# Hybrid RG-LRU and attention layer: the recurrent stage's gate multiplies and one-minus on VectorE, its input scaling on ScalarE

## The chip, the cores and the metric

The kernel runs on one core of one Trainium2 chip. The metric is device time in microseconds of one execution, the median of several runs. The profile is one execution on the chip, taken by the hardware profiler.

Names of engines, as the profile has them: PE is TensorE's matmul (PEld its weight loads), DVE is VectorE, ACT is ScalarE, POOL is GpSimd, SP is SyncE, which issues the DMAs here.

## What is computed

One layer, 4096 prompt positions and 8 single sample positions, model width 1024, all in float32:

```python
xn   = rms_norm(x, norm_pre)
proj = xn @ w_in            # columns: x_rnn 512 | g_rnn 512 | q 512 | k 128 | v 128 | g_att 512
xc   = causal_conv(x_rnn, width 4)
r, i = sigmoid(block-diagonal maps of xc)         # 8 blocks of 64
log_a = -8 * r * softplus(-lam);  a = exp(log_a)
h_t  = a_t * h_{t-1} + sqrt(1 - a_t^2) * (i_t * xc_t)
rnn_out = h * silu(g_rnn)
att_out = sliding_window_attention(q, k, v, ...) * silu(g_att)   # window 128, 8 query heads, 2 kv heads
y    = x + rms_norm(concat(rnn_out, att_out) @ w_out, norm_post)
```

## The kernel before, in words

There are three stages. Stage A (to about 480 us) normalises x, transposes it, projects the columns of x_rnn and g_rnn and runs the recurrence. Stage B (to about 1095 us) projects q, k, v and g_att and does the attention. Stage C is the output projection. Stage A and stage B overlap at their border, where the last chunks of A and the first weights and keys of B are worked at once.

Positions go in 11 chunks of 384 (the last has 256 and the 8 samples). x is held transposed, features on the 128 partitions, positions along the free axis. Each float32 product is made of three matmuls in a rounded float32 type, high by high, high by low and low by high (`mm3`, L122 to L124); so the weights and x are split into a high part (`wh`, `xh`) and a low part (`wl`, `xl`).

For one chunk `ci` stage A does, with `c` for one of four groups of 128 recurrent channels:

- `load_A(ci + 1)` (L145): three tiles `xs` of 128 rows by 1024 are loaded (L153; four buffers, three of which a chunk uses, so the second and third tile of a chunk wait until the chunk before has been transposed to the end); ACT squares and sums each (`sq`, L161); DVE adds eps (L136); POOL takes the power -1/2 (L141); then `xs` is scaled by that number per row (L166).
- `prep_A` (L170): PE transposes `xs` block by block (`pt`, L176, eight of them per chunk, three transposes each); ACT and DVE split the result into `xh` and `xl` (L179, L180), which are also stored for stage B.
- `proj_A` (L289): 48 matmuls give the channel and its gate (`pr_<ci>_<c>_1` and `_2`); the four PSUM tiles of tag "mm" hold two such pairs. ACT reads the first one out twice (`xr` L298, `xc` L302), DVE makes the convolution (L304, three per group), splits it (`xk`, L312 and L313), and makes the gate (`sg`, L318, after ACT's L316). Until ACT's L302 has read a tile, PE can't start the pair after the next in it.
- `rnn_A` (L321): six matmuls with the block-diagonal maps (`gt`), then ACT's L333, L334, L337, L338 and DVE's L339, L341, L342 and, between them, the one-minus `aa` (L340).
- `scan_A` (L345): once per chunk, ACT loads another function table and takes one square root over all four groups (`uu`, L348); then per group a multiply `ix *= uu` (L350), the scan on DVE (L352), a small copy of the last column (L355), the gate multiply `hh *= sg` (L361), and a store (L362).

The order of the program's text for one chunk is a list, `A_ORDER` (L32): P1 L P0 P2 R1 X0 R0 P3 X1 R2 X2 R3 S X3, with P for proj_A, R for rnn_A, X for two steps of prep_A of the next chunk, L for load_A of the next chunk and S for scan_A. That is not the order in which the engines get their instructions: the program is built under `tile.TileContext(nc, schedule_with_timeline_sim=True)` (L885), whose scheduler places every engine's instructions by its own model of their times. Each engine then works through its instructions in the order that the scheduler gave. So an edit of one line can shift the instructions of all the engines.

Of the kernel before, what the change touches and what calls it, by code (L numbers as in the profile page):

```python
# [12 lines left out]
AF = mybir.ActivationFunctionType  # L13
ALU = mybir.AluOpType
# [30 lines left out]
def hymba_kernel(ctx: ExitStack, tc: tile.TileContext, ins, outs):  # L45
    nc = tc.nc
# [14 lines left out]
    act = nc.scalar.activation  # L61
# [16 lines left out]
    def ps_s(n):  # L78
        if phase[0] == "A":
            return ps[1].tile([P, 1024], F32, tag="s", name=n, bufs=1)  # L80
        return ps[0].tile([P, 1024], F32, tag="s", name=n, bufs=2)
# [39 lines left out]
    def mm3(out, wh, wl, xh, xl, first, last):  # L121
        nc.tensor.matmul(out, wh, xh, start=first, stop=False)  # L122
        nc.tensor.matmul(out, wh, xl, start=False, stop=False)  # L123
        nc.tensor.matmul(out, wl, xh, start=False, stop=last)  # L124
# [10 lines left out]
    def rstd(pool, ss, rows, n):  # L135
        nc.vector.tensor_scalar(ss[:rows], ss[:rows], EPS, None, op0=ALU.add)  # L136
        return root(pool, ss, rows, n)

    def root(pool, ss, rows, n):
        rs = pool.tile([P, 1], F32, tag="rs", name=f"rs_{n}", bufs=4)  # L140
        nc.gpsimd.tensor_tensor(rs[:rows], ss[:rows], mhalf[:rows], op=ALU.pow)  # L141
        return rs


    def load_A(pool, ci):  # L145
        t0, npt, ns = chunks[ci]
        tiles = [(x_p[t0 + i * P:t0 + (i + 1) * P, :], P, i * P) for i in range(npt // P)]
        if ns:
            tiles.append((x_s, ns, npt))
        xn = []  # L150
        for j, (src, rows, off) in enumerate(tiles):
            xs = pool.tile([P, D], F32, tag="xs", name=f"xs_{ci}_{j}", bufs=4)
            nc.sync.dma_start(xs[:rows], src)  # L153
            ss = pool.tile([P, 1], F32, tag="ss", name=f"ss_{ci}_{j}", bufs=4)
            if ci == 0 and j == 1:
                sq = pal.tile([P, D], F32, tag="uu", name=f"sq_{ci}_{j}", bufs=1)
                nc.vector.tensor_tensor_reduce(sq[:rows], xs[:rows], xs[:rows], op0=ALU.mult, op1=ALU.add,
                                               scale=1.0 / D, scalar=0.0, accum_out=ss[:rows])
            else:
                sq = pool.tile([P, D], mybir.dt.bfloat16, tag="sq", name=f"sq_{ci}_{j}", bufs=1)  # L160
                act(sq[:rows], xs[:rows], AF.Square, scale=1.0 / 32.0, accum_out=ss[:rows])  # L161
            rs = rstd(pool, ss, rows, f"{ci}_{j}")
            if ci == 0:
                nc.vector.tensor_scalar(xs[:rows], xs[:rows], rs[:rows], None, op0=ALU.mult)
            else:
                nc.gpsimd.tensor_scalar(xs[:rows], xs[:rows], rs[:rows], 1.0, op0=ALU.mult, op1=ALU.mult)  # L166
            xn.append((xs, rows, off))
        return xn

# [28 lines left out]
    cms = [tc.tile_pool(name=n, bufs=1) for n in ("pa_late", "pa", "prep")]  # L198
    pal, pa, prep = [c.__enter__() for c in cms]
    xn = load_A(prep, 0)  # L200

    def project2(w1, w2, xs, W, n, wait=False):
# [118 lines left out]
    def rnn_A(pool, ci, c, uu, xc, xk, sg):  # L321
        t0, npt, ns = chunks[ci]
        W = npt + ns
        pg = ps_s(f"gt_{ci}_{c}")
        for g in range(2):
            o = pg[:, g * 512:g * 512 + W]
            mm3(o, gwh[:, 2 * c + g, :], gwl[:, 2 * c + g, :], xk[:, 0, :W], xk[:, 1, :W], True, True)

        def wt(tag, bufs=2, pool=pool):
            return pool.tile([P, STEP], F32, tag=tag, name=f"{tag}_{ci}_{c}", bufs=bufs)[:, :W]  # L330

        thr, thi = wt("thr", 3, pal), wt("thi", 4, pal)
        act(thr, pg[:, 0:W], AF.Tanh, scale=0.5, bias=hba[:, c:c + 1])  # L333
        act(thi, pg[:, 512:512 + W], AF.Tanh, scale=0.5, bias=hbx[:, c:c + 1])  # L334

        tt, aa = wt("tt", 2, pal), wt("aa", 4, pal)
        act(tt, thr, AF.Tanh, scale=sp2[:, c:c + 1], bias=sp2[:, c:c + 1])  # L337
        act(thr, thr, AF.Exp, scale=sp4n[:, c:c + 1], bias=sp4n[:, c:c + 1])  # L338
        nc.vector.scalar_tensor_tensor(thr, thr, 1.0, tt, op0=ALU.add, op1=ALU.mult)  # L339
        nc.gpsimd.tensor_scalar(aa, thr, -1.0, 1.0, op0=ALU.mult, op1=ALU.add)  # L340
        nc.vector.scalar_tensor_tensor(uu[:, c, :W], thr, 2.0, thr, op0=ALU.subtract, op1=ALU.mult)  # L341
        nc.vector.scalar_tensor_tensor(thi, thi, 1.0, xc[:, :W], op0=ALU.add, op1=ALU.mult)  # L342
        return aa, thi, sg

    def scan_A(pool, ci, uu, parts):  # L345
        t0, npt, ns = chunks[ci]
        W = npt + ns
        act(uu[:, :, :W], uu[:, :, :W], AF.Sqrt, scale=-0.25)  # L348
        for c, (aa, ix, sg) in enumerate(parts):
            nc.gpsimd.tensor_mul(ix, ix, uu[:, c, :W])  # L350
            hh = pal.tile([P, STEP], F32, tag="hh", name=f"hh_{ci}_{c}", bufs=4)
            nc.vector.tensor_tensor_scan(hh[:, :npt], aa[:, :npt], ix[:, :npt], hprev[c] if ci else 0.0,  # L352
                                         op0=ALU.mult, op1=ALU.add)
            hprev[c] = const.tile([P, 1], F32, tag=f"hl{c}", name=f"hl_{ci}_{c}", bufs=2)
            nc.gpsimd.tensor_copy(hprev[c], hh[:, npt - 1:npt])  # L355
            if ns:
                o = hh[:, npt:W]
                nc.vector.tensor_mul(o, aa[:, npt:W], h0T[:, c, :])
                nc.vector.tensor_add(o, o, ix[:, npt:W])
                nc.gpsimd.tensor_copy(hs[:, c, :], o)  # L360
            nc.gpsimd.tensor_mul(hh[:, :W], hh[:, :W], sg[:, :W])  # L361
            nc.sync.dma_start(mix_d[ci][:, c, :], hh[:, :W])  # L362


# [76 lines left out]
    for ci in range(NCH):  # L441
        for item in A_ORDER:
            f, s = item[0], st[ci]
            c = int(item[1:] or 0)
            if f == "P":
                s["p", c] = proj_A(pa, ci, c, wA, s["x"])
            elif f == "R":
                if "uu" not in s:
                    s["uu"] = pal.tile([P, 4, STEP], F32, tag="uu", name=f"uu_{ci}", bufs=1)
                s["r", c] = rnn_A(pa, ci, c, s["uu"], *s["p", c])  # L450
            elif f == "S":
                scan_A(pa, ci, s["uu"], [s["r", c] for c in range(4)])
            elif ci + 1 < NCH:
                if f == "L":
                    s["n"] = load_A(prep, ci + 1)
                else:
                    x = st[ci + 1].setdefault("x", ([], []))
                    prep_A(ci + 1, s["n"], (2 * c, 2 * c + 1), x)
        if ci == 3:
            setup_bias(pa)  # L460
# [314 lines left out]
    for ci in range(NCH):  # L775
# [14 lines left out]
        for j, (xsrc, ydst, rows, off) in enumerate(tiles):  # L790
# [52 lines left out]
            rs = root(const, ss[:, 0:1], rows, f"c{n}")  # L843
# [56 lines left out]
```

## Time and profile before

| | |
|---|---|
| runs | 1454.05, 1455.19, 1452.31 us, median 1454.05 |
| the profiled execution | 1454.09 us, of which its span is 1452.4 us |
| mean granted TensorE clock | 0.988 of full |
| busy over the span | PE 1408.3 us (97%), DVE 908.6 (63%), ACT 798.7 (55%), POOL 604.6 (42%) |
| chain that ended last, by engine | PE 83%, DVE 5%, ACT 4%, DMA 3%, issue 3%, POOL 1% |

The span is the time between the first and the last recorded instruction; 1.7 us of the execution lie outside it. An engine's busy time is the union of its instructions. The page prints the span in 40 slices, in tenths of busy time (9 is 90% or more), of which stage A is the first 13 or so:

```
PE   6999999999988889999999999999999999999998
DVE  5788777777878756576575575575665445334433
ACT  4656656666645566766776776776864222222211
POOL 3366665555656633544543543543762000000000
```

### The profile page before, as it was taken

The numbers are of one execution on the slowest core, as the hardware profiler recorded it, in microseconds if no ns is written. First come the engines' busy times: TensorE is split into PE (matmuls) and PEld (weight loads), VectorE is DVE, ScalarE is ACT, GpSimd is POOL, SyncE is SP. The second block draws the span as 40 slices with busy tenths as digits, with TensorE's granted clock in tenths as the row PEclk, the third lists the DMA queues.
The fourth block names the chain that finished last, engine by engine and source line by source line (L and its number), as shares of the span: only waits on it lengthen the run. The fifth ranks groups of instructions, "written<-read, shape, count | busy, mean of one in ns | idle before, by whom it ended". The sixth has DMA issues, their size and how long they took to land.

```text
span 1452.4 us, 24152 instructions
## 1 busy us (share of the span) xinstructions
PE 1408.3 (97%) x8127; PEld 1326.6 (91%) x8127; DVE 908.6 (63%) x2108; ACT 798.7 (55%) x2055; POOL 604.6 (42%) x1026
## 2 busy tenths in 40 slices
PE   6999999999988889999999999999999999999998
PEld 5999999999988889999999999999988888888886
DVE  5788777777878756576575575575665445334433
ACT  4656656666645566766776776776864222222211
POOL 3366665555656633544543543543762000000000
PEclk9999999999999999999999999999999999999999
DMA  8343354443324520221212212212336534433431
GB/s 271 127 157 133 131 168 148 142 152 120 122 73 145 184 79 31 99 85 67 99 46 76 98 42 79 98 38 70 107 111 196 172 131 145 141 135 131 146 130 60
DMA packets 115029, 170.24 MB, mean 117 GB/s; under 512 B 12214, under 2 KB 98822, under 8 KB 114906
## 3 DMA queue, kind: packets, MB, share of 16 engines
q1 hardware_dynamic: 114906, 168.71, 34.6%
q8 instruction: 64, 1.05, 0.3%
q14 instruction: 59, 0.48, 0.1%
HBM read 100.19 MB, written 68.50 MB: 116 GB/s over the span
## 4 chain that ended last, share of the span: by engine, by line
PE 83%; DVE 5%; ACT 4%; DMA 3%; issue 3%; POOL 1%; SPq 1%; POOLq 0%; DVEq 0%; ACTq 0%
PE out L817 8%; PE out L818 8%; PE out L819 8%; PE pr L122 6%; PE pr L124 6%; PE pr L123 6%; PE pga L122 4%; PE pga L123 4%; PE pga L124 4%; PE pq L122 4%; PE pq L123 4%; PE pq L124 4%; PE po L661 3%; PE S L601 2%; PE S L602 2%
## 5 line engine op out<-in xcount | busy, mean ns | idle before, releaser
L123 PE MATMUL pr<-xl,wh_in 128*128 128x384 f32 (+1 forms) x688 | 231.6, 337 | 0.0
L124 PE MATMUL pr<-xh,wl_in 128*128 128x384 f32 (+1 forms) x688 | 228.9, 334 | 0.0
L122 PE MATMUL pr<-xh,wh_in 128*128 128x384 f32 (+1 forms) x688 | 218.7, 336 | 0.9 <-ACT xc L302 0.6
L817 PE MATMUL out<-wh_out,xh_mix_d 128*128 128x512 f32 (+1 forms) x520 | 201.0, 387 | 0.0
L818 PE MATMUL out<-wl_out,xh_mix_d 128*128 128x512 f32 (+1 forms) x520 | 200.9, 386 | 0.0
L819 PE MATMUL out<-wh_out,xl_mix_d 128*128 128x512 f32 (+1 forms) x520 | 200.9, 386 | 0.0
L141 POOL TENSOR_TENSOR rs_c<-ssc,mhalf 128x1 f32<-128x1 f32 (+1 forms) x33 | 20.4, 620 | 322.5 <-DVE ssc L840 294.6
L836 ACT ACTIVATE sqc<-out 128x512 bf16<-128x512 f32 (+2 forms) x67 | 39.2, 585 | 194.6 <-PE out L819 184.4
L627 ACT ACTIVATE tt<-tt,nm 128x129 f32<-128x129 f32 x256 | 100.0, 393 | 77.2 <-DVE nm L624 76.7
L839 DVE TENSOR_TENSOR out<-out,gpost 128x512 f32<-128x512 f32 (+1 forms) x65 | 45.4, 698 | 144.2 <-ACT sqc L836 143.6
L123 PEld LDWEIGHTS pr<-xl,wh_in 128*128 128x128 f32 x688 | 131.3, 191 | 0.7 <-issue 0.7
L122 PEld LDWEIGHTS pr<-xh,wh_in 128*128 128x128 f32 x688 | 129.8, 191 | 2.1 <-ACT xc L302 1.8
L124 PEld LDWEIGHTS pr<-xh,wl_in 128*128 128x128 f32 x688 | 131.2, 191 | 0.3 <-issue 0.2
L122 PE MATMUL pq<-xh_B,wh_in 128*128 128x384 f32 (+1 forms) x352 | 119.5, 339 | 7.7 <-DVE kt L486 4.8
L123 PE MATMUL pga<-xl_B,wh_in 128*128 128x384 f32 (+1 forms) x352 | 119.1, 338 | 0.0
L123 PE MATMUL pq<-xl_B,wh_in 128*128 128x384 f32 (+1 forms) x352 | 118.9, 338 | 0.0
L124 PE MATMUL pq<-xh_B,wl_in 128*128 128x384 f32 (+1 forms) x352 | 118.6, 337 | 0.0
L304 DVE SCALAR_TENSOR_TENSOR xc<-xr,cT,xc 128x384 f32<-128x384 f32 (+1 forms) x132 | 113.0, 862 | 8.6 <-ACT xc L302 5.9
L122 PE MATMUL pga<-xh_B,wh_in 128*128 128x384 f32 (+1 forms) x352 | 118.3, 336 | 0.0
L124 PE MATMUL pga<-xh_B,wl_in 128*128 128x384 f32 (+1 forms) x352 | 117.5, 334 | 0.0
L817 PEld LDWEIGHTS out<-wh_out,xh_mix_d 128*128 128x128 f32 x520 | 97.6, 188 | 19.8 <-issue 0.2
L819 PEld LDWEIGHTS out<-wh_out,xl_mix_d 128*128 128x128 f32 x520 | 97.7, 188 | 19.6
(258 smaller groups left out, 3711.2 us busy)
## 6 DMA issues: line engine op xcount, KB each, us to landing
xs<-in_x_prompt_dram SPq DMA_DIRECT2D x32, 512.0 KB
xr<-in_x_prompt_dram SPq DMA_DIRECT2D x32, 512.0 KB
out_dram<-xr SPq DMA_DIRECT2D x31, 512.0 KB
xT_d<-xh SPq DMA_DIRECT2D x80, 192.0 KB
xT_d<-xl SPq DMA_DIRECT2D x80, 192.0 KB
xf_mix_d<-mix_d SPq DMA_DIRECT2D x80, 192.0 KB
xh_B<-xT_d SPq DMA_DIRECT2D x80, 192.0 KB
xl_B<-xT_d SPq DMA_DIRECT2D x80, 192.0 KB
```

The lines of the kernel that those rows point to most:

```text
L122: nc.tensor.matmul(out, wh, xh, start=first, stop=False)
L123: nc.tensor.matmul(out, wh, xl, start=False, stop=False)
L124: nc.tensor.matmul(out, wl, xh, start=False, stop=last)
L304: nc.vector.scalar_tensor_tensor(xc[:, :npt], xr[:, t:t + npt], cw[:, t, c:c + 1], xc[:, :npt], op0=ALU.mult, op1=ALU.add)
L601: nc.tensor.matmul(o, qa, kt[:, kv, 0, kr], start=True, stop=False)
L627: act(tt[:, g, 0:P + 1], tt[:, g, 0:P + 1], AF.Exp, scale=-1.0, bias=nm[:, g:g + 1], accum_out=sm[:, g:g + 1])
L661: nc.tensor.matmul(pog[:, :, r], v.rearrange("p l d -> p (l d)"), w[:, :, r], start=i == 0, stop=i == 2)
L817: nc.tensor.matmul(p, a, wh, start=st, stop=False)
L818: nc.tensor.matmul(p, a, wl, start=False, stop=False)
L819: nc.tensor.matmul(p, b, wh, start=False, stop=sp)
L836: act(sq[:rows, :c[1] - c[0]], p[:rows], AF.Square, scale=1.0 / 32.0, accum_out=ss[:rows, i:i + 1])
L839: nc.vector.tensor_mul(po[i][:rows], p[:rows], gpost[:rows, c[0]:c[1]])
```

## The change

Four instructions of stage A get another engine. The scaling of `xs` for chunks 1 to 10 (L166, 29 tiles of 128x1024 and one of 8x1024) goes from POOL to ACT, as a Copy with a scale per row. The one-minus (L340) and the two multiplies (L350, L361), 44 of each, go from POOL to DVE. POOL keeps the power (L141), the small copies (L295, L300, L310, L355, L360), six weight lows that it makes (L112), and what it does in stage B.

```diff
@@ load_A
             if ci == 0:
                 nc.vector.tensor_scalar(xs[:rows], xs[:rows], rs[:rows], None, op0=ALU.mult)
             else:
-                nc.gpsimd.tensor_scalar(xs[:rows], xs[:rows], rs[:rows], 1.0, op0=ALU.mult, op1=ALU.mult)
+                act(xs[:rows], xs[:rows], AF.Copy, scale=rs[:rows])
             xn.append((xs, rows, off))
@@ rnn_A
         nc.vector.scalar_tensor_tensor(thr, thr, 1.0, tt, op0=ALU.add, op1=ALU.mult)
-        nc.gpsimd.tensor_scalar(aa, thr, -1.0, 1.0, op0=ALU.mult, op1=ALU.add)
+        nc.vector.tensor_scalar(aa, thr, -1.0, 1.0, op0=ALU.mult, op1=ALU.add)
@@ scan_A
         for c, (aa, ix, sg) in enumerate(parts):
-            nc.gpsimd.tensor_mul(ix, ix, uu[:, c, :W])
+            nc.vector.tensor_mul(ix, ix, uu[:, c, :W])
@@ scan_A
-            nc.gpsimd.tensor_mul(hh[:, :W], hh[:, :W], sg[:, :W])
+            nc.vector.tensor_mul(hh[:, :W], hh[:, :W], sg[:, :W])
             nc.sync.dma_start(mix_d[ci][:, c, :], hh[:, :W])
```

The scheduler places the whole of stage A anew. Three places follow, each first as before and then as changed. In the names, the first number after a tile's name is the chunk (`xs_8_1` is the second tile of chunk 8), the last is the program's own count.

ACT around the square root of chunk 6, before: the end of the recurrent gates of chunk 6, the table, the square root `uu_6`, the two squares of chunk 8's tiles, and the reading out of `pr_7_1_1`.

```order
L338 ACTIVATE thr_6_3_3687<-thr_6_3_3687,sp4n_257 128x384
L179 ACTIVATE xh_7_6_3732<-pt_7_6_3728,gpre_148 128x384
L179 ACTIVATE xh_7_7_3742<-pt_7_7_3738,gpre_148 128x384
L348 ACT_TABLE_LOAD
L348 ACTIVATE uu_6_3495<-uu_6_3495 128x1536
L161 ACTIVATE sq_8_1_3827,ss_8_1_3826<-xs_8_1_3824 128x1024
L161 ACTIVATE sq_8_2_3836,ss_8_2_3835<-xs_8_2_3833 128x1024
L298 ACTIVATE xr_7_1_3798<-pr_7_1_1_3748 128x384
L302 ACTIVATE xc_7_1_3803<-pr_7_1_1_3748,cT_250 128x384
```

ACT at the same place in the changed kernel:

```order
L179 ACTIVATE xh_7_6_3732<-pt_7_6_3728,gpre_148 128x384
L179 ACTIVATE xh_7_7_3742<-pt_7_7_3738,gpre_148 128x384
L338 ACTIVATE thr_6_3_3687<-thr_6_3_3687,sp4n_257 128x384
L161 ACTIVATE sq_8_1_3827,ss_8_1_3826<-xs_8_1_3824 128x1024
L348 ACT_TABLE_LOAD
L348 ACTIVATE uu_6_3495<-uu_6_3495 128x1536
L161 ACTIVATE sq_8_2_3836,ss_8_2_3835<-xs_8_2_3833 128x1024
L166 ACTIVATE xs_8_1_3824<-xs_8_1_3824,rs_8_1_3830 128x1024
L298 ACTIVATE xr_7_1_3798<-pr_7_1_1_3748 128x384
L302 ACTIVATE xc_7_1_3803<-pr_7_1_1_3748,cT_250 128x384
```

The square of `xs_8_1`, which needs that tile's load, now stands ahead of the table and the square root, and the new scaling L166 stands ahead of the reading out of `pr_7_1_1`.

PE before `pr_7_2_1`, the first product in the PSUM tile that `pr_7_1_1` was in, before the change:

```order
L124 MATMUL pr_7_0_2_3843<-xh_7_7_3742,wl_in4_302 128x384
L176 MATMUL pt_8_0_3996<-ident_101,xs_8_0_3815 128x128
L176 MATMUL pt_8_1_4006<-ident_101,xs_8_0_3815 128x128
L122 MATMUL pr_7_2_1_3909<-xh_7_0_3519,wh_in2_307 128x384
L123 MATMUL pr_7_2_1_3909<-xl_7_0_3520,wh_in2_307 128x384
```

PE at the same place in the changed kernel:

```order
L124 MATMUL pr_7_0_2_3843<-xh_7_7_3742,wl_in4_302 128x384
L176 MATMUL pt_8_0_3996<-ident_101,xs_8_0_3815 128x128
L176 MATMUL pt_8_1_4006<-ident_101,xs_8_0_3815 128x128
L176 MATMUL pt_8_0_3996<-ident_101,xs_8_1_3824 128x128
L176 MATMUL pt_8_1_4006<-ident_101,xs_8_1_3824 128x128
L122 MATMUL pr_7_2_1_3909<-xh_7_0_3519,wh_in2_307 128x384
L123 MATMUL pr_7_2_1_3909<-xl_7_0_3520,wh_in2_307 128x384
```

The two transposes of `xs_8_1` have come up from behind the whole of `pr_7_2` and `gt_7_1`. Between the first transpose of `pt_7_7` and this place PE has 49 matmuls of `pr` before the change and 42 after it.

PE at the gates of chunk 9 near the end of stage A, before:

```order
L123 MATMUL pr_9_2_2_4872<-xl_9_7_4705,wh_in6_313 128x384
L124 MATMUL pr_9_2_2_4872<-xh_9_7_4704,wl_in6_314 128x384
L122 MATMUL gt_9_1_4939<-xk_9_1_4770,gwh_291 128x384
L123 MATMUL gt_9_1_4939<-xk_9_1_4770,gwh_291 128x384
L124 MATMUL gt_9_1_4939<-xk_9_1_4770,gwl_292 128x384
```

PE at the same gates in the changed kernel:

```order
L124 MATMUL pr_9_3_2_4998<-xh_9_2_4587,wl_in7_326 128x384
L122 MATMUL pr_9_3_1_4997<-xh_9_3_4597,wh_in3_319 128x384
L123 MATMUL pr_9_3_1_4997<-xl_9_3_4598,wh_in3_319 128x384
L124 MATMUL pr_9_3_1_4997<-xh_9_3_4597,wl_in3_320 128x384
L122 MATMUL gt_9_1_4939<-xk_9_1_4770,gwh_291 128x384
L122 MATMUL pr_9_3_2_4998<-xh_9_3_4597,wh_in7_325 128x384
```

`gt_9_1` stood directly behind `pr_9_2` and now stands behind 21 matmuls of `pr_9_3`, which don't need it.

## Rows read from the trace of the kernel before

**Rows 1.** Windows of 50 us; columns: busy PE, PEld, DVE, ACT, POOL, clock, DMA.

```profile
300.00:350.00 50.00, 49.95 (x298) 49.42 (x297) 41.33 (x68) 33.19 (x58) 28.27 (x37) 1.00 0.40 139
450.00:500.00 50.00, 40.33 (x246) 38.66 (x245) 42.35 (x72) 28.72 (x52) 39.22 (x45) 0.89 0.57 177
```

**Rows 2.** PE's waits from 50 to 400 us: total us, times, longest.

```profile
PE pr L122 <- ACT xc L302: 0.6, 1, 0.6
PE gt L123 <- DVE xk L313: 0.5, 1, 0.5
```

**Rows 3.** PE's waits from 400 to 560 us.

```profile
PE gt L122 <- DVE xk L312: 6.4, 2, 3.9
PE pq L122 <- DVE kt L486: 4.8, 1, 4.8
PE S L601 <- DVE sq L566: 3.5, 1, 3.5
...
PE S L601 <- DVE nm L622: 1.0, 1, 1.0
```

**Rows 4.** Groups of POOL, 0 to 480 us: busy us, mean ns, idle before.

```profile
L350 POOL TENSOR_TENSOR thi<-thi,uu 128x384 f32<-128x384 f32 x40 | 51.8, 1326 | 23.9 <-ACT uu L348 23.9
L361 POOL TENSOR_TENSOR hh<-hh,sg 128x384 f32<-128x384 f32 x40 | 49.4, 1246 | 0.0
L166 POOL TENSOR_SCALAR xs<-xs,rs 128x1024 f32<-128x1024 f32 x29 | 41.1, 1416 | 0.3
...
L340 POOL TENSOR_SCALAR aa<-thr 128x384 f32<-128x384 f32 x40 | 27.0, 675 | 106.8 <-DVE thr L339 106.8
```

**Rows 5.** Groups of DVE, 0 to 480 us.

```profile
L304 DVE SCALAR_TENSOR_TENSOR xc<-xr,cT,xc 128x384 f32<-128x384 f32 x120 | 102.8, 863 | 8.6 <-ACT xc L302 5.9 <-POOL aa L340 2.6
...
L313 DVE TENSOR_TENSOR xk<-xc,xk 128x384 fp32r<-128x384 f32 x40 | 22.5, 563 | 0.3
```

**Rows 6.** Groups of ACT, 0 to 480 us.

```profile
L111 ACT ACTIVATE wh_in<-ws_in 128x1024 fp32r<-128x1024 f32 x10 | 10.6, 1060 | 10.1 <-DMA ws_in<-in_w_in_dram 9.7 <-PE pr L123 0.4
```

**Rows 7.** Timeline of SP at chunk 6: start, us, line, op.

```profile
317.26 0.81 SPq L153 DMA_DIRECT2D xs<-in_x_prompt_dram  x2
```

**Rows 8.** Timeline of ACT at chunk 6: start, us, line, op, idle before.

```profile
318.47 1.28 ACT L348 ACT_TABLE_LOAD   x1
319.77 1.49 ACT L348 ACTIVATE uu<-uu 128x1536 f32<-128x1536 f32 x1
321.52 1.06 ACT L161 ACTIVATE sq<-xs 128x1024 bf16<-128x1024 f32 x1 [0.26 <-DMA xs<-in_x_prompt_dram]
...
323.35 1.06 ACT L161 ACTIVATE sq<-xs 128x1024 bf16<-128x1024 f32 x1 [0.68 <-DMA xs<-in_x_prompt_dram]
...
324.41 0.47 ACT L298 ACTIVATE xr<-pr 128x384 f32<-128x384 f32 x1
324.78 0.67 ACT L302 ACTIVATE xc<-pr,cT 128x384 f32<-128x384 f32 x1
```

**Rows 9.** Timeline of PE at chunk 6.

```profile
316.63 0.82 PE L176 MATMUL pt<-ident,xs 128*128 128x128 f32 x6
...
325.80 0.38 PE L176 MATMUL pt<-ident,xs 128*128 128x128 f32 x2
325.94 0.42 PE L122 MATMUL pr<-xh,wh_in 128*128 128x384 f32 x1
```

**Rows 10.** Windows around PE's waits, columns as in rows 1.

```profile
408.00:415.60 7.60, 7.60 (x44) 7.32 (x43) 7.60 (x6) 1.42 (x5) 7.60 (x13) 1.00 0.14 52
415.60:419.90 4.30, 0.51 (x3) 0.22 (x2) 4.30 (x8) 1.04 (x3) 2.81 (x5) 1.00 0.15 54
420.30:427.20 6.90, 6.90 (x24) 6.19 (x23) 5.79 (x12) 3.10 (x6) 0.93 (x2) 0.51 0.25 82
...
519.40:526.10 6.70, 5.58 (x19) 5.58 (x20) 5.15 (x17) 5.46 (x22) 0.00 (x0) 0.50 0.01 2
1059.20:1061.00 1.80, 0.00 (x0) 0.00 (x0) 0.77 (x2) 1.78 (x10) 0.00 (x0) 1.00 0.84 257
1062.00:1065.40 3.40, 3.40 (x19) 3.40 (x17) 1.62 (x4) 2.09 (x6) 1.51 (x2) 0.51 0.00 0
```

## The prediction

> **What bounds the kernel now.** I read the busy times first: PE is busy for 97% of the span, so nothing that another engine saves is worth anything unless PE waits for it, and any new wait of PE is paid in full. So I cut the span into windows. In the steady part of stage A PE is busy 49.95 of 50 us at the full clock, with DVE at 41.33, ACT at 33.19 and POOL at 28.27 [rows 1]. At the border of stages A and B, from 450 to 500 us, it is busy 40.33 of 50 at a clock of 0.89. Next the waits. From 50 to 400 us PE waits 1.1 us for DVE and ACT together [rows 2]; there is nothing to gain there. From 400 to 560 us it waits 6.4 us for `xk` in two waits, 4.8 for the keys' low part, 3.5 and 1.0 for the first scores [rows 3], 15.7 us in all. Each long wait costs more than itself: after the wait at 415.6 us (0.51 us busy of 4.30) the granted clock was 0.51, the lower of the two levels, for 6.90 us with 24 matmuls, where just before 44 took 7.60 us [rows 10]. At 7.60 / 44 = 0.173 us each, 24 need 4.15, so that stretch lost 2.75 us.
>
> Then I looked for slack in the steady part, at chunk 6. The loads of `xs_8_1` and `xs_8_2` are issued at 317.26 [rows 7], when PE has transposed their buffers' old contents. ACT loads the table, takes the square root to 321.26, then waits for the first load (landed at 321.52, 4.26 us after issue) and the second, and reads `pr_7_1_1` out by L302, done at 325.45 [rows 8]. PE needs that tile at 325.94 [rows 9]. **That leaves about half a microsecond**, on the one queue to which the change adds work.
>
> **The change part by part.**
>
> *POOL loses* L350, L361, L166 and L340, 51.8 + 49.4 + 41.1 + 27.0 = 169 us [rows 4]. PE waits for none of them directly in the steady part, so by itself that is worth nothing there.
>
> *DVE gains* 132 instructions. The nearest row is L313, the same shape with two inputs, 563 ns [rows 5]; L340 has one input, so that is an upper bound: at most 132 x 0.563 = 74 us over 480 us, 7.7 us in 50. Against it, DVE is now slowed beside POOL: L304, of L313's shape, takes 863 ns in the mean, 0.3 us x 120 = 36 us more than at 563 [rows 5]. If that goes, DVE stands at about 41.3 + 7.7 - 3.7 = 45 of 50 us; if not, at 49. I take 45, since the POOL work that stood beside it is gone, and cost it at nothing in the steady part.
>
> A rule speaks for this part. The Trainium skill, SBUF — State Buffer, section Who interferes with whom, says that a VectorE instruction with two SBUF inputs and a GpSimd instruction that reads SBUF exclude each other for a whole instruction. By it all of L304's excess comes back to DVE; what it gives the sum is still only what PE waits for, 0.5 us of the steady part, and the border.
>
> *ACT gains* L166. The nearest row is L111, a Copy of 128x1024 at 1.06 us [rows 6]: 30 x 1.06 = 32 us, 3.2 per chunk, on an engine at 33 of 50 us. The load is harmless; its place is not. In the changed order ACT has, for chunks 1 to 8 alike, the square of `xs_..._1` (which waits for the load) ahead of the table and the square root, and L166 ahead of L298 and L302. Before, the table and the square root ran while the load was under way, and POOL did the scaling. Now they come one after the other. From the issue of the load for chunk 6, with durations from start to start: load 4.26 [rows 7, 8]; first square 1.15; table 1.28 and square root 1.45; second square 1.1; L166 1.0; L298 0.4; L302 0.67 [rows 6, 8]. The sum is 11.3 us. PE has 42 matmuls from the transposes that free the buffer to `pr_7_2_1`, 42 x 0.173 = 7.3 us. **So PE stops for 4.0 us**: about 3 ahead of the two transposes of `xs_8_1` that now stand there and need L166, and 0.9 ahead of `pr_7_2_1`, which needs L302. Before, 49 matmuls (8.5 us) covered the way from the load's issue to L302 at 8.2 (325.45 - 317.26).
>
> The other chunks by the same count: 42 matmuls in chunks 5 to 8, 43 in 3 and 4, 45 in 2, 46 in 1; chunk 4 has no second square in the chain (1.1 less). That gives 4 x 4.0 + 3.8 + 2.8 + 3.5 + 3.3 = 29; I take 28, as the wait for a landed load is seen a little late. The bounds: if a load had landed at once, 4.0 less each, the stall is next to none; a load as late as the second one, 6.1 us (323.35 - 317.26), adds 1.8 each, 43 in all. One row shows 4.26 and it is the same load, so I take that. What waits behind ACT: L316's gate, DVE's convolution and `gt`, which all move later with PE and are not late against it.
>
> Why the squares were cheap before is seen in rows 8. The Trainium skill, Perfetto Trace Analysis, section Tensor Engine Instruction, states that the queues of ScalarE, VectorE and GpSimd are strictly first in, first out. By that rule the square root can't pass a square that waits for its load; the trace agrees, for L298 started only behind the second square, which had waited 0.68 us [rows 8].
>
> *The clock after these stops.* All four long waits at the border were followed by a stretch at the lower level (two of them are shown) [rows 10], and so was one of 1.8 us near 1060, for 3.40 us. By 2.75 / 6.90 such a short stretch costs 1.4. For eight stops that is 0 (none falls) to 22 (each like the one at 420). I take 8 x 1.9 = 15, between the two prices.
>
> *The border.* `gt_9_1` gets 21 matmuls (3.6 us) ahead of it, which covers most of its 3.8 us of idling; with the clock behind it that is 6.5 us. In ACT's order the last query of the first attention chunk now stands ahead of the first exponentials instead of behind them, so the waits of 3.5 and 1.0 should go with a stretch of 2.75: 7.2. The second `xk` wait (3.9) and the keys' (4.8) I leave: `xk_10_1` has more DVE work ahead of it, the weight lows that collide with DVE stay on POOL, and the weights of stage B load ahead of its x. New small waits, by estimate 2. That is -12; the bounds are 0, and -27 if all 15.7 and four stretches of 2.75 go.
>
> *The sum:* 1454.1 (the profiled execution, which equals the median of the runs) + 28 + 15 - 12 = **1485 us**, 2.1% slower. A measurement tells 0.2%, 2.9 us, from no change.
>
> **The rivals.**
>
> *Faster: the contention was the cost.* GpSimd's slow instructions held DVE up at the border, and in the steady part ACT's longer chain doesn't stop PE. The Trainium skill, GPSIMD Engine Reference, section Engine selection, has elementwise work with two inputs on VectorE, since GpSimd is about twice as slow; the trace agrees (1246 to 1326 against 563 ns). For it: PE's waits at the border are for DVE. Against it: the order in which ACT and PE get their work is fixed, and the chain of 11.3 us would have to shrink to 7.3, which is to say that the load takes no time. It decides below a mean stop of 1.5 us a chunk. Price: the border's -12 alone, 1442; at its best 1427. Chance 0.14.
>
> *The stops come without the clock.* Each is cut in two by the transposes, and PE isn't idle for as long on end as at 460 or 493. 1454 + 28 - 12 = 1470. Chance 0.20.
>
> *About the same.* The load lands so early, or stops and border cancel so well, that the two are within 3 us of each other: stops of 1.5 us, no clock. 1454. Chance 0.06.
>
> *DVE becomes the bound.* If the slowing beside POOL doesn't go, DVE has 49 of 50 us to do, and `gt` waits for `xk` in most chunks besides: another 2 us in each of ten, 1505. Against it: the same instructions then have less POOL work beside them. Chance 0.08.
>
> **How the numbers follow.** The forecast (stops and clock, 1472 to 1500) has 0.52. The range goes from 1451 to 1503: it leaves out the faster rival and the upper half of the last, and takes in the bounds of the stops (3 to 4 us each) and of the clock (0 to 22). Faster by more than 0.2%: 0.14; within: 0.06; slower: 0.52 + 0.20 + 0.08 = 0.80.
>
> **What would show it.** In the changed profile PE should have waits of about 3 us `pt` <- ACT `xs` L166 and of 0.9 `pr` <- ACT `xc` L302, eight times, some 40 us apart, each followed by a window at a clock near 0.5; ACT's first square should start at the landing of the load, and the table right behind it; L304's mean should fall toward 0.6 us; the wait at `gt_9_1` should be gone. I am wrong if PE's windows in the steady part stay at 49.9 of 50, or if the waits there are for DVE.

## The result, and the profile after

| | before | changed |
|---|---|---|
| median of the runs | 1454.05 us | 1466.21 us (1462.05 to 1467.49) |
| ratio, 95% interval | | 1.0076, 1.0054 to 1.0098 |
| profiled execution, span | 1452.4 us | 1464.0 us |

The changed kernel is 0.8% slower, 12 us. The forecast was slower by 31 us, 1485; the range began at 1451, so the time lies in it, but the amount is off by more than half.

PE's windows of the changed kernel; the columns are those of [rows 1], and the second and third lines answer to them:

```profile
100.00:150.00 50.00, 48.24 (x287) 47.42 (x286) 35.87 (x74) 32.82 (x56) 7.43 (x16) 1.00 0.37 131
...
300.00:350.00 50.00, 47.38 (x260) 46.55 (x259) 36.10 (x73) 32.96 (x55) 13.70 (x20) 0.92 0.35 122
...
450.00:500.00 50.00, 43.13 (x295) 40.99 (x294) 39.63 (x75) 28.59 (x49) 20.52 (x20) 0.93 0.52 163
```

The steady part, which had lost nothing, now loses 2.6 us of PE and some of the clock in 50 us (260 matmuls where it did 298); the border of the stages does 295 matmuls where it did 246. The changed kernel's waits of PE, from 50 to 400 us, which answer to [rows 2]:

```profile
PE pt L176 <- ACT xs L166: 9.6, 6, 2.4
PE pr L122 <- ACT xc L302: 6.0, 7, 2.3
```

and from 400 to 560 us, which answer to [rows 3]:

```profile
PE gt L122 <- DVE xk L312: 5.5, 1, 5.5
PE pt L176 <- ACT xs L166: 2.1, 1, 2.1
PE pga L122 <- DVE sq L567: 1.4, 1, 1.4
PE pq L122 <- DVE kt L486: 1.4, 1, 1.4
...
PE pr L122 <- ACT xc L302: 0.5, 1, 0.5
```

Both waits named in the forecast are there: the one for L302 behind each of chunks 1 to 8, the one for L166 behind all of them but chunk 3. Together PE is idle in them for 9.6 + 6.0 + 2.1 + 0.5 = 18.2 us. In place of the 15.7 us of [rows 3] stand 8.3. With the small waits, which neither list shows in full, the border has 10.2 us of waits besides the stops, where it had 17.8.

The chain at chunk 6 in the changed kernel, first SP (the load's issue), then ACT, then PE:

```profile
332.60 0.81 SPq L153 DMA_DIRECT2D xs<-in_x_prompt_dram  x2
```

```profile
336.58 1.06 ACT L161 ACTIVATE sq<-xs 128x1024 bf16<-128x1024 f32 x1 [2.27 <-DMA xs<-in_x_prompt_dram]
...
337.75 1.28 ACT L348 ACT_TABLE_LOAD   x1
339.05 1.49 ACT L348 ACTIVATE uu<-uu 128x1536 f32<-128x1536 f32 x1
340.44 1.04 ACT L161 ACTIVATE sq<-xs 128x1024 bf16<-128x1024 f32 x1
...
341.48 1.13 ACT L166 ACTIVATE xs<-xs,rs 128x1024 f32<-128x1024 f32 x1
342.51 0.47 ACT L298 ACTIVATE xr<-pr 128x384 f32<-128x384 f32 x1
342.88 0.66 ACT L302 ACTIVATE xc<-pr,cT 128x384 f32<-128x384 f32 x1
```

```profile
339.91 0.38 PE L176 MATMUL pt<-ident,xs 128*128 128x128 f32 x2
342.66 0.69 PE L176 MATMUL pt<-ident,xs 128*128 128x128 f32 x2 [2.37 <-ACT xs L166]
343.60 0.69 PE L122 MATMUL pr<-xh,wh_in 128*128 128x384 f32 x1 [0.25 <-ACT xc L302]
344.08 0.52 PE L123 MATMUL pr<-xl,wh_in 128*128 128x384 f32 x1
344.40 0.52 PE L124 MATMUL pr<-xh,wl_in 128*128 128x384 f32 x1
```

ACT sits for 2.27 us in front of a square whose load is under way, with the table and the square root behind it; compare [rows 8], where those two ran in that time. From issue to the end of L302 it takes 10.9 us (343.54 - 332.60). Two transposes take 0.14 us here when nothing holds them [rows 9], so PE could have begun `pr` at 340.19 and began at 343.60: 3.4 us. After it, the products start 0.32 us apart instead of 0.173: the granted clock is 0.50 there, until 349 us. The window behind the stop at chunk 5, which holds such a stretch and the rise after it, shows 0.58:

```profile
298.70:302.00 3.30, 3.29 (x11) 3.29 (x12) 3.30 (x5) 3.29 (x6) 3.30 (x5) 0.58 0.00 0
```

DVE's groups from 0 to 480 us in the changed kernel, which answer to [rows 4, 5]:

```profile
L304 DVE SCALAR_TENSOR_TENSOR xc<-xr,cT,xc 128x384 f32<-128x384 f32 x120 | 70.6, 610 | 6.0 <-ACT xc L302 5.9
...
L352 DVE TENSOR_TENSOR_SCAN hh<-aa,hl,thi 128x384 f32<-128x384 f32 x35 | 33.2, 999 | 0.0
...
L350 DVE TENSOR_TENSOR thi<-thi,uu 128x384 f32<-128x384 f32 x40 | 21.8, 608 | 23.6 <-ACT uu L348 23.6
...
L361 DVE TENSOR_TENSOR hh<-hh,sg 128x384 f32<-128x384 f32 x36 | 19.1, 546 | 0.1
L340 DVE TENSOR_SCALAR aa<-thr 128x384 f32<-128x384 f32 x40 | 14.3, 357 | 0.9
```

The scan L352 in the profile of before, from 0 to 480 us:

```profile
L352 DVE TENSOR_TENSOR_SCAN hh<-aa,hl,thi 128x384 f32<-128x384 f32 x36 | 55.5, 1563 | 2.7 <-POOL thi L350 2.7
```

DVE took over three kinds of instruction and is still less busy in the steady part than before, 36 of 50 us against 41. A part of that is that PE hands it less work in the window, 260 matmuls for 298. The rest is that its instructions are shorter: L304 fell from 863 to 610 ns, the scan from 1563 to 999, and the cast L312 from 673 to 352.

### The profile page after: what moved, and what is told of

Its sections match the earlier page's. It is cut to its first block, busy times and chain, and to the rows that moved or that the text cites. A ratio compares the mean times of both kernels' runs of the same rounds, so it can differ in the third digit from the quotient of the medians.

```text
span 1464.0 us, 24094 instructions
## 1 busy us (share of the span) xinstructions
PE 1410.0 (96%) x8127; PEld 1326.7 (91%) x8127; DVE 895.6 (61%) x2240; ACT 828.3 (57%) x2085; POOL 450.3 (31%) x864
## 4 chain that ended last, share of the span: by engine, by line
PE 84%; ACT 6%; DMA 4%; DVE 3%; issue 1%; SPq 1%; POOL 0%; POOLq 0%; DVEq 0%; ACTq 0%
PE out L817 8%; PE out L818 8%; PE out L819 8%; PE pr L122 7%; PE pr L123 6%; PE pr L124 6%; PE pga L122 4%; PE pga L123 4%; PE pga L124 4%; PE pq L122 4%; PE pq L123 4%; PE pq L124 4%; PE po L661 3%; DMA xs<-in_x_prompt_dram 2%; DMA ws_in<-in_w_in_dram 2%; PE S L601 2%
## 5 line engine op out<-in xcount | busy, mean ns | idle before, releaser
L122 PE MATMUL pr<-xh,wh_in 128*128 128x384 f32 (+1 forms) x688 | 223.8, 342 | 8.8 <-ACT xc L302 6.9
L141 POOL TENSOR_TENSOR rs_c<-ssc,mhalf 128x1 f32<-128x1 f32 (+1 forms) x33 | 20.4, 619 | 322.3 <-DVE ssc L840 293.9
L818 PEld LDWEIGHTS out<-wl_out,xh_mix_d 128*128 128x128 f32 x520 | 97.7, 188 | 19.2
```

The lines of the kernel that those rows point to most:

```text
L818: nc.tensor.matmul(p, a, wl, start=False, stop=False)
```

## The experiments

Each run's ratio is to the kernel before, with the 95% interval. Theory Q below is the forecast's: the order of ACT's queue makes the stops. Its rivals: the scaling itself (S), DVE's new work (D), too few buffers (B).

### The parts one at a time

**e1_scale_only**, the change's L166 alone:

```diff
-                nc.gpsimd.tensor_scalar(xs[:rows], xs[:rows], rs[:rows], 1.0, op0=ALU.mult, op1=ALU.mult)
+                act(xs[:rows], xs[:rows], AF.Copy, scale=rs[:rows])
```

> The kernel before with one part of the change: only the scaling of xs (L166) goes from POOL to ACT; the gate multiplies and the one-minus stay on POOL. The scheduler leaves ACT's order around the square root as before: table, square root, the two squares, L298 and L302, and L166 after them. Theory Q (the stops of the changed kernel come from ACT's order, in which a square that waits for its load stands ahead of the table and the square root): no stops, PE waits under 2 us from 50 to 400 us, the border of stages A and B about as before, 1454 us, 1450 to 1458. Rival S (the scaling's 1.1 us on ACT, three times a chunk, is what makes ACT late, wherever it stands): stops in every chunk, 1462 to 1468. Rival D (the work that DVE takes over makes the stops): no stops here, 1454.

1448.73 us, 0.9963 (0.995 to 0.9977). The only wait of PE from 50 to 400 us is one of 0.8 us:

```profile
PE pr_rev L402 <- POOL anti L398: 0.8, 1, 0.8
```

So 32 us more work on ACT stops nothing by itself; theory S falls. It is a little faster than expected, 1 us below the range. A part of that shows at the border: before, POOL's L166 stands beside DVE's L304 at 410.65 and 413.96 us; here it doesn't, and the two waits of `gt_9_1`, 2.5 and 1.3 us before, are 1.5 and 0.6.

**e2_gates_only**, the three lines that go to DVE, without L166:

```diff
-        nc.gpsimd.tensor_scalar(aa, thr, -1.0, 1.0, op0=ALU.mult, op1=ALU.add)
+        nc.vector.tensor_scalar(aa, thr, -1.0, 1.0, op0=ALU.mult, op1=ALU.add)
...
-            nc.gpsimd.tensor_mul(ix, ix, uu[:, c, :W])
+            nc.vector.tensor_mul(ix, ix, uu[:, c, :W])
...
-            nc.gpsimd.tensor_mul(hh[:, :W], hh[:, :W], sg[:, :W])
+            nc.vector.tensor_mul(hh[:, :W], hh[:, :W], sg[:, :W])
```

> The kernel before with the other part: the gate multiplies and the one-minus (L340, L350, L361) go to DVE, the scaling L166 stays on POOL. In the order that the scheduler gives, a square stands ahead of the square root behind chunks 2, 3, 6, 7 and 8, and behind it after chunks 1, 4 and 5. Theory Q: PE stops in those five chunks and not in the other three; without L166 in the chain each stop is about 1 us shorter than the 1.7 to 2.6 us of the changed kernel, so 5 to 8 us with what the clock takes; the border gains about what it gained in the changed kernel (16 us): 1445 us, 1438 to 1452. Rival S: no stops at all, 1436 to 1440. Rival D: stops in all chunks, as in the changed kernel, with PE waiting for DVE: 1462 to 1468.

1456.60 us (1450.22 to 1463.98), 1.0019 (0.9998 to 1.0039): nearly 5 us above the expected range. PE's waits from 50 to 400 us:

```profile
PE pr L122 <- ACT xc L302: 6.7, 5, 2.0
PE pt L176 <- POOL xs L166: 0.4, 1, 0.4
```

The waits for L302 lie behind chunks 2, 3, 6, 7 and 8 (1.7, 0.6, 1.4, 2.0 and 1.4 us), and behind none of 1, 4 and 5, as the order says; one of 1.0 behind chunk 0 I had not looked for. What PE waits for in the steady part is ACT, so theory D falls. The total missed, as far as the runs show, for two reasons. At the border this kernel has waits that neither the kernel before nor the changed one has (4.0 us for `xk` L313, 3.8 for ACT's `thi` L334). And the clock is not the same in every execution: in the profiled one, 1450.22 us at a mean clock of 0.994, no stop before 450 us is followed by a stretch at the lower level; others took 1456.18 at 0.989 and 1463.98 at 0.986. So the gates on DVE alone make the scheduler put a square ahead of the square root behind five chunks, where L166 alone (e1_scale_only) does so behind none. Only both together do it behind all eight.

### The order alone

**f1_root_first**, the whole change, with the squares held behind the square root on ACT by an edge that sets the order and no wait:

```diff
+    roots, reads = {}, {}
+
+    def behind(ins):
+        return tc.issue_after(getattr(ins, 'ins', ins)) if ins is not None else ExitStack()
...
-                act(sq[:rows], xs[:rows], AF.Square, scale=1.0 / 32.0, accum_out=ss[:rows])
+                with behind(roots.get(ci - 2) if j else None):
+                    act(sq[:rows], xs[:rows], AF.Square, scale=1.0 / 32.0, accum_out=ss[:rows])
...
-        act(uu[:, :, :W], uu[:, :, :W], AF.Sqrt, scale=-0.25)
+        roots[ci] = act(uu[:, :, :W], uu[:, :, :W], AF.Sqrt, scale=-0.25)
```

> The whole change, with one thing held: an order-only edge on ACT keeps each chunk's squares behind the square root of two chunks earlier. ACT's order is then table, square root, the first square, L298, L302, and L166 comes after them, while DVE, POOL and ACT do the same work as in the changed kernel. Theory Q: the stops go, PE waits under 2 us from 50 to 400 us, and the gain at the border stays: 1438 us, 1434 to 1444, faster than both kernels. Rival S: ACT still has the scaling, so the stops stay, 1460 to 1468. Rival D: DVE still has the multiplies, so the stops stay, 1460 to 1468.

1433.21 us (1432.18 to 1435.32), 0.9847 (0.9831 to 0.9864): faster than both kernels, and a little below the expected range. The trace has no wait of PE from 50 to 400 us. Its window, and ACT at chunk 6 (line numbers are six higher in this kernel):

```profile
300.00:350.00 50.00, 50.00 (x301) 49.69 (x300) 38.28 (x79) 34.78 (x60) 13.61 (x17) 1.00 0.37 127
```

```profile
318.27 1.28 ACT L354 ACT_TABLE_LOAD   x1
319.74 1.49 ACT L354 ACTIVATE uu<-uu 128x1536 f32<-128x1536 f32 x1 [0.18 <-DVE uu L347]
321.13 1.04 ACT L167 ACTIVATE sq<-xs 128x1024 bf16<-128x1024 f32 x1
...
322.32 0.50 ACT L304 ACTIVATE xr<-pr 128x384 f32<-128x384 f32 x1
322.71 0.67 ACT L308 ACTIVATE xc<-pr,cT 128x384 f32<-128x384 f32 x1
```

The square no longer waits: its load lands under the table and the square root. All engines do the work of the changed kernel; only the order differs. The edge moves the squares, and with them more falls back into the place that it had before the change: L166 comes after L302, and PE's transposes of `xs_8_1` come after `pr_7_2_1` (only one pair, at 323.86, stands ahead of it). So f1_root_first undoes this whole part of the order, and what the stops cost is 1464.0 - 1433.6 = 30.4 us of span. At the border the two kernels differ a little besides: f1_root_first has no wait of 1.4 us at `pga`, and a stretch of 3.4 us more at the lower clock. What is left of the change is worth 1433.6 - 1452.4 = -18.8.

**f3_order_of_after**, the reverse: e1_scale_only, which has no stops, put into the changed kernel's order:

```diff
+    def put_behind(late, early):
+        tc.add_manual_dep(getattr(late, 'ins', late), getattr(early, 'ins', early).name,
+                          mybir.DependencyInfo(mybir.DependencyClass.NoSync, mybir.DependencyReason.DATA),
+                          reason="order")
...
-                act(sq[:rows], xs[:rows], AF.Square, scale=1.0 / 32.0, accum_out=ss[:rows])
+                got = act(sq[:rows], xs[:rows], AF.Square, scale=1.0 / 32.0, accum_out=ss[:rows])
+                if j == 1 and ci - 2 in roots:
+                    put_behind(roots[ci - 2], got)
...
+                got = act(xs[:rows], xs[:rows], AF.Copy, scale=rs[:rows])
+                if j == 1 and ci > 1:
+                    put_behind(reads[ci - 1], got)
```

(`roots` holds the square roots as above, `reads` the L298 of each chunk's first group.)

> The kernel of run e1_scale_only (only the scaling on ACT, 1448.7 us, no stops) with ACT's order around the square root forced to that of the changed kernel by two order-only edges: square, table, square root, square, scaling, L298, L302. No engine does other work than in e1_scale_only, and DVE none of the multiplies. PE has 56 matmuls from the freeing of the buffer to pr_2 (53 behind chunk 3), 9.7 us at 0.173; the chain took 10.9 us in the changed kernel. Theory Q (order): eight stops of about 1.2 us, 10 us in all, with 0 to 8 us of clock: 1461 us, 1456 to 1468. Rival D (the multiplies on DVE are needed for the stops): no stops, 1447 to 1452.

1486.82 us, 1.0231 (1.0211 to 1.0251), 38 us above e1_scale_only. The stops come without any multiply on DVE, but the time is 19 us past the range. PE's waits from 50 to 400 us (L325 and L326 are the `xk` lines here, L175 the scaling, L315 `xc`):

```profile
PE gt L122 <- DVE xk L325: 8.3, 5, 1.7
PE pt L187 <- ACT xs L175: 7.1, 7, 1.5
PE pr L122 <- ACT xc L315: 4.5, 8, 1.1
PE gt L123 <- DVE xk L326: 3.6, 6, 0.7
```

The second and third line are the expected stops, 11.6 us (2.0 of it behind chunk 0, where none was expected; 1.5 more, behind chunk 8, come after 400 us). The first and fourth, 11.9 us, I had not reckoned with: a late square root makes the multiplies and the scans late too, and here the multiplies are on POOL. DVE's scans then take

```profile
351.31 4.94 DVE L365 TENSOR_TENSOR_SCAN hh<-aa,hl,thi 128x384 f32<-128x384 f32 x3
```

for three, beside POOL's L363 from 350.24 for 5.20 us, and they stand ahead of the convolution that `gt` needs. In the changed kernel, where DVE does both, PE never waited for `xk` in that part. This suggests that moving the multiplies to DVE kept the stops from being dearer. It is not shown, since the two kernels' orders differ in other places too, and the rest of the 19 us (the border's waits for `xk` alone are 8.4 us against 5.4 in e1_scale_only) was not taken apart.

### What makes up a stop

**f4_scale_behind**, the whole change, with L166 of a chunk's later tiles behind L302 of its first group; the square stays ahead:

```diff
-                act(xs[:rows], xs[:rows], AF.Copy, scale=rs[:rows])
+                with behind(reads.get(ci - 1) if j else None):
+                    act(xs[:rows], xs[:rows], AF.Copy, scale=rs[:rows])
```

(here `reads` holds L302 of the first group.)

> The whole change, with the scaling of the later tiles held behind L302 of the chunk's first group by an order-only edge; the square stays ahead of the table and the square root. The chain from the load's issue to L302 loses the scaling's 1.0 us: 9.9 us; PE has 47 to 51 matmuls there, 8.1 to 8.8 us, and no transposes of the new tile. Theory Q: eight stops of 1.1 to 1.8 us, all pr waiting for L302, 11 us in all, and 0 to 6 us of clock, on top of the 1433 us of the run without stops: 1447 us, 1442 to 1452. A theory in which the scaling alone makes the stops: 1433 us. One in which only the square's place counts: as the changed kernel, 1462 to 1467.

1449.63 us, 0.9972 (0.996 to 0.9983). PE's waits from 50 to 400 us:

```profile
PE pr L122 <- ACT xc L308: 9.7, 6, 2.0
```

With one more of 2.0 at 420 that is 11.7 us against 11 expected, in seven stops instead of eight (none behind chunk 4, which has no second square in the chain), and the waits at `pt` are gone, since PE's transposes of the new tile stand behind `pr` here too. The chain can thus be taken apart: with what the clock takes, L166's place and that of those transposes are worth 16.6 us (1466.2 to 1449.6) and the square's the other 16.4 (1449.6 to 1433.2).

**e4_xs6**, the whole change with six buffers:

```diff
-            xs = pool.tile([P, D], F32, tag="xs", name=f"xs_{ci}_{j}", bufs=4)
+            xs = pool.tile([P, D], F32, tag="xs", name=f"xs_{ci}_{j}", bufs=6)
```

> The whole change with six buffers for xs instead of four, so that every tile is loaded one tile-set earlier and PE never waits for a tile of the coming chunk. The square ahead of the square root is then that of a tile of the chunk after, whose load is still issued only when PE has transposed the old contents. Theory Q: the square root still waits for a load of about 4 us, so PE stops nearly as before, now at pr for L302 alone, behind chunks 1 to 7 but not behind 8, where the square root stands first: 12 to 18 us of waits, 1458 to 1466. Rival B (PE stops because the tiles that it transposes come too late, for want of buffers): no stops, 1436 to 1442.

1464.35 us, 1.0063 (1.0048 to 1.0078), no real gain on the changed kernel. From 50 to 400 us:

```profile
PE pr L122 <- ACT xc L302: 19.8, 7, 3.8
```

PE's own tiles are there in time; it stops because ACT waits for a load that PE doesn't need yet. Theory B falls. At 19.8 us, the waits are a little above the 12 to 18 that I expected.

### What the rest is worth

**f5_root_first_pool**, f1_root_first with L166 back on POOL:

```diff
-                act(xs[:rows], xs[:rows], AF.Copy, scale=rs[:rows])
+                nc.gpsimd.tensor_scalar(xs[:rows], xs[:rows], rs[:rows], 1.0, op0=ALU.mult, op1=ALU.mult)
```

> The kernel of run f1_root_first (1433.2 us) with the scaling L166 back on POOL; the multiplies and the one-minus on DVE, the square root ahead of the squares. Theory Q: no stops in 50 to 400 us, so the time differs from 1433 only by what the border gives: 1430 to 1442, 1436. If moving the scaling to ACT is worth something by itself (POOL's L166 beside DVE's convolution), this is slower than f1_root_first by 3 us or more; if ACT is short, faster.

1439.96 us, 0.9906 (0.9891 to 0.9921), 6.7 us above f1_root_first. So the two halves, where the squares stand behind the root, are worth -5.5 (L166, e1_scale_only) and -13.9 (the rest, this run), and together -21.0 (f1_root_first): they nearly add up. But in this run PE waits for POOL's scaling, twice before 400 us for 1.5 us in all, where no stop was expected, and once behind it for 3.2 us:

```profile
PE pt L182 <- POOL xs L172: 3.2, 1, 3.2
```

**f6_lows_on_dve**, f1_root_first with the weight lows of stage B on DVE:

```diff
-            wB[m] = load_w_in(m, eng=nc.gpsimd) if len(wB) < 8 else load_w_in(m, pbl, 2, eng=nc.gpsimd)
+            wB[m] = load_w_in(m) if len(wB) < 8 else load_w_in(m, pbl, 2)
```

> The kernel of run f1_root_first with the weight lows of stage B (L112) on DVE instead of POOL. In that run PE waits 5.5 us at the gates of the last chunk for xk, and DVE has two instructions of 2.6 and 2.3 us there beside POOL's L112 of 2.85 and 2.59, where the same take 0.47 and 0.21 alone. If that collision makes the wait, it shrinks by 2 to 4 us, less the 1.2 us that each L112 costs DVE, and with it perhaps the clock's fall behind it: 1430 us, 1426 to 1433. If DVE's queue itself is the bound there, no faster: 1433 to 1437.

1434.09 us, 0.9869 (0.9853 to 0.9885): no faster than f1_root_first. The wait of 5.5 us for `xk` is gone, and with it DVE's two long instructions, as the collision theory says. But the scheduler has placed PE's instructions anew there too, and PE now waits elsewhere at the border:

```profile
PE pk L122 <- ACT vt L550: 2.8, 1, 2.8
PE S L607 <- DVE nm L628: 2.8, 1, 2.8
PE po L650 <- issue: 1.4, 1, 1.4
PE gt L122 <- ACT thi L340: 1.2, 1, 1.2
```

From 400 to 560 us its waits are 9.8 us in all, where f1_root_first has 8.7. f1_root_first stays the best version.

## Why the forecast was right and wrong

**Right: the mechanism, its place and its sign.** The half microsecond of slack on ACT's queue was the thing to look at. The stops came in all eight chunks named, at the two instructions named (behind chunk 3 only at the second), and behind the cause named: f1_root_first takes it away with one edge, f3_order_of_after makes it where there was none. The rule of the forecast that ScalarE's queue is strictly first in, first out (the Trainium skill, Perfetto Trace Analysis, section Tensor Engine Instruction) agrees with the trace of the changed kernel: at chunk 6 the table and the square root started only behind the square that had waited 2.27 us.

**Wrong: three sizes, all in the same direction.** The second and third of the measured ones are differences of spans: the clock is what is left of the 30.4 us behind the stops.

| term | forecast | measured |
|---|---|---|
| the eight stops | +28 | +22.4 |
| the clock after them | +15 | about +8 |
| the border and the rest | -12 | -18.8 |
| sum | +31 | +11.6 (spans) |

*The stops.* Counted as at chunk 6 (from where PE could have begun `pr` to where it did), they are 2.3, 2.9, 2.4, 2.2, 3.0, 3.4, 3.1 and 3.2 us. Two steps failed. One is "load 4.26": I took one load's time from before for all eight. In the changed kernel the first square of a chunk started 3.5 to 4.0 us after issue, 3.7 in the mean, which is 0.5 us x 8 = 4 us. The other is PE's own way, "42 x 0.173 = 7.3 us": it left out the transposes of `xs_..._0` and `xs_..._1`, which stand in it too. That way took 7.6 us in each of chunks 5 to 8 (340.19 - 332.60 at chunk 6), and over all eight chunks it was about 3 us longer than counted. The 29 less these 7 is what was measured; the 1 us taken off for a load that "is seen a little late" rests on no row. The other links were right: square, table, root, square, scaling and two readings took 7.0 us at chunk 6 (336.58 to 343.54), and the forecast had 7.05.

*The clock.* The step "8 x 1.9" assumed that every stop is followed by a stretch at the lower level, at a price between two seen. Six of the eight were, five for 3.4 us and one for 6.8 by the granted clock in the trace, and in three of them a part had passed before PE's products went on. The spans leave 30.4 - 22.4 = 8.0 us. Counted in the trace, 73 products started in 22.0 us of these stretches, which at 0.173 us would take 12.6: about 9 us, 1.5 a stretch. The time came out near that of the rival without the clock, 1470, but not for its reason.

*The border.* The waits of 3.5 and 1.0 for the first scores went as forecast, and `gt_9_1` too. What failed is the step "and the keys' (4.8) I leave": that wait fell to 1.4. In the changed kernel three of the four stretches at the lower level went with the waits, where the forecast took off about two; with the 7.6 us less of waits that is some 16 of the 18.8, by an estimate of 2.75 a stretch. The 3.9 for the last chunk's `xk`, which I left too, grew to 5.5. f5_root_first_pool and e1_scale_only show that both halves of the change have a share in this gain. How much of it is DVE freed from POOL's neighbourhood and how much is the other order of instructions there was not separated; f6_lows_on_dve, in which one such collision goes and the time doesn't fall, is a warning against the first alone.

*DVE's load* was wrong too, though it cost nothing: 45 of 50 us were forecast, 36 were measured, and 38 in the same window of f1_root_first, where PE keeps its full pace (301 matmuls). The forecast gave back only L304's excess (36 us forecast, 0.25 x 120 = 30 measured). The scan's (about 22 us over 40 scans) and the cast's (0.32 x 40 = 13) were left out, and the moved one-minus took 357 ns, not 563.

On the pages that speak for the change: the Trainium skill, GPSIMD Engine Reference, section Engine selection (GpSimd about twice as slow on two inputs) agrees, 1326 and 1246 ns against 608 and 546. By the rule in the Trainium skill, SBUF — State Buffer, section Who interferes with whom, all of the excess of L304 and the scan beside POOL should come back with POOL's work gone. The traces agree: the fastest single instructions before took 0.59 us (L304) and 0.94 to 1.00 us (the scan), and 610 and 999 ns are the means after.

The rival "faster: the contention was the cost" failed on its condition, that ACT's longer chain stops nothing. Where that is forced, in f1_root_first, the time is 1433, between its 1442 and its best of 1427.

## What to carry to other kernels

When a scheduler places the instructions, an edit that moves work between engines is two edits: the work, and a new order on every queue. Read the new order at the place with the least slack, and ask of each in-order queue what stands behind an instruction that waits for a load. Here one order-only edge was worth 33 us, more than all that the moves gained, and turned a loss of 12 us into a gain of 21.

A stop's size is the difference of two long ways, so errors of half a microsecond in either matter; take a load's time from several loads, and both ways instruction by instruction.

## What the runs showed of the hardware that I had not expected

One program, with the same instructions in the same order, spread over 13.8 us (e2_gates_only, 1450.22 to 1463.98 us) with its mean granted clock between 0.994 and 0.985: in the profiled execution, the fastest, none of its stops of 0.6 to 2.0 us was followed by a stretch at 1.2 GHz; the others weren't traced, but their lower mean clock says that more of their time fell to that level. In the changed kernel's profiled execution the stops behind chunks 1 and 4 (2.3 and 2.2 us, cut in two by a pair of transposes) were not followed by one, and the six others were, that of chunk 3 among them, 2.4 us in one piece. In e4_xs6 all seven stops, of 2.1 to 3.8 us in one piece, were followed by one; in f4_scale_behind the three of 1.9 to 2.0 us were, and the four of 1.1 to 1.7 us were not.

The scan on DVE lost more time per instruction to POOL's work than DVE's other kinds that were compared (L304, L312, L341): 1563 ns before, 1578 with only L166 gone from POOL (e1_scale_only), 1058 with only the multiplies and the one-minus gone (e2_gates_only), 999 with both, and 1771 in f3_order_of_after, where the multiplies stand right beside the scans. L304 got a part back from each: 863 ns before, 684 in e1_scale_only, 680 in e2_gates_only, 610 with both.
